# Splitting half of each plain weight quad by ScalarE and accumulating transfers in the last halves of an MLP, and an eighth mixed pair

## The chip, the cores and the metric

The kernel runs on one core of a Trainium2 chip. The metric is device time in microseconds (us) of one execution. Before the change three runs took 1934.14, 1934.61 and 1934.19 us, median 1934.19 us.

## The reference

A trunk of two layers on 256 tokens of width 2048, all in float32. Layer 0 mixes tokens by a convolution module, layer 1 by latent attention; behind each stands a squared-ReLU MLP, and the change lies in its second product alone:

```
def sq_relu_mlp(h, w1, w2):
    return jnp.square(jax.nn.relu(h @ w1)) @ w2      # 256x2048 @ 2048x8192, then @ 8192x2048
...
    h = rms_norm(x, norm_mlp_g[layer])
    x = x + sq_relu_mlp(h, mlp_w1[layer], mlp_w2[layer])
return rms_norm(x, final_norm_g)
```

## The kernel before, in words

**Split operands.** TensorE multiplies float32r operands, so each float32 value is held as a rounded upper part and a lower part. ScalarE writes the upper part of a weight tile (`hi`), VectorE subtracts it from the loaded weights (`raw`) and writes the lower part (`lo`). `mm3` (L203 to L205) makes one product of three matmuls: upper by upper, lower input by upper weight, upper input by lower weight, in this order.

**The MLP** (`mlp`, L609) runs in two halves of the 8192 hidden columns. A half has an up product (L655, L656: eight groups g of four hidden chunks of 128) and then a down product. The turned, normalised input of the up product stands in the tiles `xt`; in the last half nobody reads it after the up product. Between the two, each finished group is squared and split (L673 to L687).

**The down product of a half** has 32 chunks of 128 rows of w2, taken in pairs: 16 pairs. The output has four column blocks of 512, and two of them are made together by one `Sums` (n = 0, then n = 2). One pair by two column blocks is a *quad*: one load of 1 MB on SP's queue into one of three `raw` buffers. A quad is either

- *plain* (`Sums.plain`, L559): 8 products of `mm3`, so 24 matmuls, with two tiles of 128x1024 split by L170 (ScalarE) and L174 (VectorE); or
- *mixed* (`Sums.mixed`): 7 products, so 21 matmuls, by sums of weight blocks and of input blocks that make a 2x2 block product out of seven. Its weight blocks are prepared by `mixed_weights` (L490): four splits (L497 ScalarE, L498 VectorE) and three differences made in `raw` by VectorE (L505, L506, L507).

`MIXED` lists which pairs are mixed: eight of 16 in three of the four halves, and seven (0, 1, 4, 5, 8, 9, 12) in the last half of layer 1. `HEAD` and `TAIL` keep plain quads at both ends of a `Sums`; in n = 0 the order is two plain, two mixed, plain, two mixed, plain and so on. I call the quads of one `Sums` p0, p1, ... (plain) and m0, m1, ... (mixed).

In the last half of layer 1 the second `Sums` (n = 2) is made by `product_A` (L417), which takes plain chunks in units of four rows by one column block, so that columns 2 and 3 end one after the other; `between` puts the mixed quads among the units of column block 2. Behind it come the residual adds and the final norm.

**What sets the order.** The tile framework gives each engine its own order of instructions; an engine takes them in that order and waits by semaphores. The buffers set how far VectorE and ScalarE run ahead of TensorE: six `hi` and six `lo` tiles (`WB`), three `raw` buffers (`load`, L153). SP issues a load when the last reader of the buffer's earlier content is done. Transfers that add into what stands in SBUF are issued by GpSimd (POOL); before the change it issues them only in `Sums.put` (L578), for sums of 128x512.

Of the kernel before, what the change touches and what calls it, by code (L numbers as in the profile page):

```python
# [10 lines left out]
F32 = mybir.dt.float32  # L11
# [27 lines left out]
PAD_RIGHT = 48  # L39
PAD_KV = 8  # L40
PAD_O = 56
WB = 6
# [37 lines left out]
def trunk_kernel(  # L80
# [335 lines left out]

    def product_A(  # L417
        w, k_lo, nk, hi, lo, add, prepare, blocks=range(NNB), due=(), finish=None, before=None,
        units=None, banks=None, begun=None, beside=None, room=None,
    ):  # L420

        due = list(due)
        units = [list(range(4 * u, 4 * u + 4)) for u in range(nk // 4)] if units is None else units
        begun = set() if begun is None else begun
        nu = len(units)

        def first(ps):
            fresh = id(ps) not in begun
            begun.add(id(ps))
            return fresh  # L430

        for n in blocks:
# [12 lines left out]
            for u, ks in enumerate(units):  # L445
                if u == 0 and beside is not None:
                    beside(n, -1, due)
                wjs.append(load_split([rows(w, k_lo + ks[0], len(ks), n * NB, NB)], len(ks)))
                if u < nu - n_end:
                    for j, k in enumerate(ks):  # L450
                        for t in range(T):
                            mm3(ps[t], hi(k, t), lo(k, t), *wjs[u](j), first(ps[t]), u == nu - 1 and k == ks[-1])
                if banks is None:
                    while due:
                        prepare(due.pop(0))
                    step(-(-20 * 4 // nk) + 1 if nk > 4 * NNB else 6)
                elif n == blocks[-1]:
                    for _ in range(len(due) if n_end else min(1, len(due))):
                        prepare(due.pop(0), out=room)
                if beside is not None:  # L460
                    beside(n, u, due)
            if n_end:
                before()
                for t in range(T):


                    halves = t == T - 1
                    for u in range(nu - n_end, nu - halves):
                        products(u, t, not halves)
                    add(n, ps, t)  # L470
                    if not halves:
                        prepare(n, t)
                    else:
                        h = NB // 2
                        for c in range(2):
                            o = acc_tile()[:, :h]
                            for j, k in enumerate(units[-1]):
                                wh, wl = (w[:, c * h : (c + 1) * h] for w in wjs[-1](j))
                                mm3(o, hi(k, t), lo(k, t), wh, wl, j == 0, k == units[-1][-1])
                            add(n, {t: o}, t, c)  # L480
                            prepare(n, t, c)
                    finish(t)
            else:
                for t in range(T):
                    add(n, ps, t)
                due.append(n)
        while due:
            prepare(due.pop(0))
# [23 lines left out]
    def mixed_inputs(v, fh, fl):  # L512
# [15 lines left out]
        nc.vector.tensor_tensor(a12, a12, a11, op=ALU.subtract)  # L528
        halves(a, 3, 4)

    class Sums:


# [25 lines left out]
        def plain(self, w, k, hi, lo, k0, end, middle=None):  # L559

            at_j = split(load([rows(w, k, 2, self.n * NB, 2 * NB)], 2), nc.vector)
            order = [(j, c, t) for j in range(2) for c in range(2) for t in range(T)]
            if end:
                order.sort(key=lambda r: r[1:])
            for i, (j, c, t) in enumerate(order):
                if middle is not None and 2 * i == len(order):
                    middle()
                wh, wl = (a[:, c * NB : (c + 1) * NB] for a in at_j(j))
                ps = self.e[t][c]
                mm3(ps, hi(k0 + j, t), lo(k0 + j, t), wh, wl, self.first(ps), end and j == 1)  # L570
# [34 lines left out]
                        self.put(t, c, o)  # L605

    put_off = []

    def mlp(layer, ssq, next_gain, finish=None, before=None, beside=None, after_up=None):  # L609

        with ExitStack() as cx:
# [22 lines left out]
            for hf in range(HALVES):  # L634
# [72 lines left out]
                split_end = last and finish is not None  # L707
                for n in range(0, NNB - 2 * split_end, 2):
                    sums = Sums(n, not last or split_end)
                    ks = [2 * p for p in ps]  # L710
                    at, head = 0, HEAD[n // 2]
                    for i, k in enumerate(ks):
                        upto = (len(ms) * (i - head + 1) + (head > 1) * (len(ks) - head - TAIL)) // (len(ks) - head - TAIL + 1)
                        while at < min(upto, len(ms)):
                            mixed_quad(sums, at)
                            at += 1
                        if i == len(ks) - TAIL + 1:
                            sums.join(room)
                        at_end = i == len(ks) - 1
                        sums.plain(  # L720
                            w, k_lo + k, hi, lo, k, at_end,
                            (lambda: [prepare(due.pop(0), out=room, rest=rest) for _ in range(len(due))]) if at_end else None,
                        )
                    sums.close(room)
                    while rest:
                        rest.pop(0)()
                    if last:
                        due += [n, n + 1]
                if last and not split_end:
                    put_off.extend(lambda n=n: prepare(n) for n in due)  # L730
                if split_end:
                    sums = Sums(NNB - 2, False)
                    n2 = NNB - 2
                    units = [list(range(4 * g, 4 * g + 4)) for g in plain]
                    units[1:1] = [[2 * p, 2 * p + 1] for p in ps if p // 2 in mixed]
                    nu, at_ = len(units), [0]

                    def between(n, u, due):
                        if n == n2 and u < nu - 1:
                            while at_[0] < min(len(ms), -(-len(ms) * sum(map(len, units[: u + 1])) // sum(map(len, units[:-1])))):  # L740
                                mixed_quad(sums, at_[0])
                                at_[0] += 1
                        if n == n2 and u == nu - 1:
                            sums.join(room)

                    if after_up is not None:
                        after_up()
                    product_A(
                        w, k_lo, nkh, hi, lo, add, prepare, range(n2, NNB), due,
                        finish=(lambda t: finish(nssq, t)) if finish is not None else None,  # L750
                        before=lambda: before(nssq),
                        units=units, banks={n2 + c: [sums.e[t][c] for t in range(T)] for c in range(2)},
                        begun=sums.begun, beside=between, room=room,
                    )
            return nssq

# [1099 lines left out]
    with ExitStack():  # L1856
        gfs = []

        def load_gf():
            gfs.append(right_pool("gf", 1).tile([P, D], F32, name="gf"))  # L1860
# [83 lines left out]
```

## Time and profile before

| | |
|---|---|
| runs, median | 1934.19 us |
| the profiled execution, from its first to its last instruction | 1932.5 us |
| TensorE (PE) busy | 1921.0 us |
| VectorE (DVE), ScalarE (ACT), GpSimd (POOL) busy | 1592.2, 1095.6, 249.0 us |
| read from HBM | 363.68 MB |
| last half of layer 0: up product, down product | 641.3 to 818.8 us, 818.8 to about 980 us |
| last half of layer 1: up product, down product and end | 1582.3 to 1759.8 us, 1759.8 to 1932.5 us |

The profile has one row for an engine, a group of equal instructions or a stretch of time. A row of the timeline gives start, duration, engine, line, operation, out<-in, and in brackets the engine's idle time before it with what ended it. Times count from the start of the span. Matmuls overlap: a row of 0.39 us starts some 0.23 us after the one before it.

### The profile page before, as it was taken

What the parts mean: (1) busy time and instruction counts of PE and PEld (TensorE: products, weight loads), DVE (VectorE), ACT (ScalarE), POOL (GpSimd) and SP (SyncE); (2) the same over time, 40 slices, a digit from 0 to 9 for tenths busy, and PEclk for the clock granted to TensorE, in tenths of its full rate; (3) what the DMA queues carried; (4) which work ended last, traced back from release to release, by engine and by line L of the source; (5) the groups of instructions that cost most, each with busy time, mean ns of one, the idle gap of its engine ahead of it and who ended that gap; (6) DMA issues with size and microseconds to landing.
All of it is one profiled execution on the core that took longest, in us unless ns stands there. A gap on an engine that the chain in (4) does not pass through costs nothing.

```text
span 1932.5 us, 28477 instructions
## 1 busy us (share of the span) xinstructions
PE 1921.0 (99%) x10725; PEld 1681.5 (87%) x10725; DVE 1592.2 (82%) x2457; ACT 1095.6 (57%) x1636; POOL 249.0 (13%) x208
## 2 busy tenths in 40 slices
PE   9999999999999999999999999999999999999998
PEld 8999888888888888888898998888888888888887
DVE  7999988877999776799976766877789987678998
ACT  5667755554555545555576655555555554455554
POOL 6999200000010100000001420000000010000000
PEclk9999999999999999999999999999999999999999
DMA  7766456665585866655656545465646776665774
GB/s 230 214 183 189 153 189 206 193 194 177 175 251 194 263 195 187 194 174 196 217 176 175 142 134 192 155 216 186 188 162 225 222 248 212 191 196 175 231 219 150
DMA packets 230427, 375.50 MB, mean 194 GB/s; under 512 B 16392, under 2 KB 107792, under 8 KB 230032
## 3 DMA queue, kind: packets, MB, share of 16 engines
q1 hardware_dynamic: 224640, 363.28, 58.7%
q0 software_dynamic: 4320, 7.87, 2.2%
q10 hardware_dynamic: 1328, 2.52, 0.4%
q8 instruction: 84, 1.38, 0.3%
q14 instruction: 55, 0.45, 0.1%
HBM read 363.68 MB, written 2.10 MB: 189 GB/s over the span
## 4 chain that ended last, share of the span: by engine, by line
PE 97%; DVE 2%; DMA 0%; ACT 0%; issue 0%; ACTq 0%; DVEq 0%
PE acc L655 24%; PE acc L205 15%; PE acc L203 15%; PE acc L204 15%; PE acc L656 13%; PE acc L823 8%; PE acc L1287 2%; DVE sum L910 1%; DMA xs<-in_x 0%; PE acc L1535 0%; PE acc L1566 0%; PE acc L1565 0%; PE acc L1536 0%; PE acc L1564 0%; PE acc L1537 0%; PE tr L267 0%
## 5 line engine op out<-in xcount | busy, mean ns | idle before, releaser
L174 DVE TENSOR_TENSOR lo<-raw,hi 128x1024 fp32r<-128x1024 f32 (+2 forms) x509 | 602.2, 1197 | 232.3 <-ACT hi L170 226.6
L170 ACT ACTIVATE hi<-raw 128x1024 fp32r<-128x1024 f32 (+2 forms) x574 | 583.9, 1036 | 361.1 <-PE acc L655 203.7
L655 PE MATMUL acc<-xt,hi 128*128 128x512 f32 x2048 | 710.6, 390 | 0.0
L656 PE MATMUL acc<-xt,lo 128*128 128x256 f32 x2048 | 577.5, 282 | 0.0
L655 PEld LDWEIGHTS acc<-xt,hi 128*128 128x128 f32 x2048 | 384.3, 188 | 80.7
L656 PEld LDWEIGHTS acc<-xt,lo 128*128 128x128 f32 x2048 | 387.1, 189 | 0.2
L497 ACT ACTIVATE hi<-raw 128x1024 fp32r<-128x1024 f32 x248 | 228.7, 948 | 228.3 <-DVE raw L505 134.0
L498 DVE TENSOR_TENSOR lo<-raw,hi 128x1024 fp32r<-128x1024 f32 x248 | 263.9, 1087 | 27.6 <-ACT hi L497 22.5
L203 PE MATMUL acc<-hi,sh 128*128 128x512 f32 x514 | 200.1, 389 | 0.0
L205 PE MATMUL acc<-lo,sh 128*128 128x512 f32 x514 | 200.1, 389 | 0.0
L203 PE MATMUL acc<-hi,gh 128*128 128x512 f32 (+1 forms) x516 | 200.0, 388 | 0.0
L205 PE MATMUL acc<-lo,gh 128*128 128x512 f32 (+1 forms) x516 | 199.9, 387 | 0.0
L204 PE MATMUL acc<-hi,gl 128*128 128x512 f32 (+1 forms) x516 | 199.9, 387 | 0.0
L823 PE MATMUL acc<-xt,hi 128*128 128x256 f32 x1024 | 180.2, 281 | 0.3 <-ACT b L1106 0.2
L204 PE MATMUL acc<-hi,sl 128*128 128x512 f32 x450 | 175.1, 389 | 0.0
L578 POOL DMA_DIRECT2D xs<-v x30 | 26.5, 994 | 1136.4 <-DVE lo L174 703.2
L910 DVE SCALAR_TENSOR_TENSOR sum<-ub,w_dw,sum 128x256 f32<-128x256 f32 x409 | 164.3, 481 | 3.6 <-ACT sum L880 3.0
L174 POOL TENSOR_TENSOR lo<-raw,hi 128x1024 fp32r<-128x1024 f32 x65 | 155.0, 2410 | 17.3 <-ACT hi L170 17.3
L823 PEld LDWEIGHTS acc<-xt,hi 128*128 128x128 f32 x1024 | 154.8, 188 | 1.1 <-ACT xt L1090 0.6
L823 PE MATMUL acc<-xt,lo 128*128 128x256 f32 x512 | 139.2, 279 | 0.0
L205 PEld LDWEIGHTS acc<-lo,sh 128*128 128x128 f32 x514 | 96.5, 188 | 20.4 <-DVE lo L498 0.3
L204 PEld LDWEIGHTS acc<-hi,gl 128*128 128x128 f32 x516 | 96.9, 188 | 19.9
(314 smaller groups left out, 2531.3 us busy)
## 6 DMA issues: line engine op xcount, KB each, us to landing
raw<-in_mlp_w SPq DMA_DIRECT2D x255, 1024.0 KB, 5.5
raw<-in_conv_w_pw SPq DMA_DIRECT2D x62, 512.0 KB, 5.1
raw<-in_conv_w_pw SPq DMA_DIRECT2D x16, 1024.0 KB, 5.1
raw<-in_mla_w_o SPq DMA_DIRECT2D x16, 1024.0 KB, 5.7
raw<-in_mla_w_kv_up SPq DMA_DIRECT2D x32, 256.0 KB, 3.9
xs<-v POOLq DMA_DIRECT2D x30, 256.0 KB, 7.8
raw<-in_mla_w_in SPq DMA_DIRECT2D x8, 576.0 KB, 3.8
raw<-in_mla_w_in SPq DMA_DIRECT2D x4, 1024.0 KB
```

Source lines behind the costliest of these rows:

```text
L170: nc.scalar.activation(hi, raw[:, js, :], AF.Copy)
L174: eng.tensor_tensor(lo, raw, hi.bitcast(F32), op=ALU.subtract)
L203: nc.tensor.matmul(ps, sh, mh, start=start, stop=False)
L204: nc.tensor.matmul(ps, sl, mh, start=False, stop=False)
L205: nc.tensor.matmul(ps, sh, ml, start=False, stop=stop)
L497: nc.scalar.activation(hi, src, AF.Copy)
L498: nc.vector.tensor_tensor(lo, src, hi.bitcast(F32), op=ALU.subtract)
L655: nc.tensor.matmul(ps[b], wh[:, bs], xhl(k), start=k == 0, stop=False)
L656: nc.tensor.matmul(ps[b][:, :S], wl[:, bs], xh(k), start=False, stop=k == KC - 1)
L823: nc.tensor.matmul(pss[c][b][:, :S], w[i][:, bs], (xh, xl)[j](k), start=k == i + j == 0, stop=end and k == k0 + nk - 1 and (i, j) == terms ...
L910: nc.vector.scalar_tensor_tensor(out=out, in0=ubs[c][:, w : w + S], scalar=tap(c, w), in1=base, op0=ALU.mult, op1=ALU.add)
L1287: nc.tensor.matmul(ps2[b][t], x_kt(k, t), w[:, bs], start=k == g == i == 0, stop=k == KC - 1 and i == len(group) - 1,)
```

## The change

Four edits, all in the last half of each layer's MLP, except the table's:

1. `MIXED`: the last half of layer 1 gets pair 13 as an eighth mixed pair.
2. `side_parts`: for a plain quad, the second of its two tiles is no longer split through `hi` and `lo`. ScalarE writes -raw, rounded, into `l`; GpSimd issues a transfer that reads the same weights from HBM again and adds them onto `l`, which leaves the lower part; ScalarE writes the upper part `h` in a second operation. The first tile is split as before.
3. This is done one quad ahead in the program: `side_parts` of a plain quad, its load too, stands before the quad that precedes it. p0 is left out, and in layer 0's n = 2 the last two. In layer 1's `product_A` the three plain units behind mixed quads of column block 2 are done so, each before the mixed quad that precedes it. These are 12 quads in layer 0 and 10 in layer 1.
4. `h` and `l` (tags sideh, sidel; three buffers each) stand where `xt` stood; `xt` is opened again for the next stage in layer 0, and the final gain `gf` moves into the same pool in layer 1.

```diff
-MIXED = {(layer, half): (0, 1, 4, 5, 8, 9, 12) + (13,) * (layer + half < 2) for layer in range(2) for half in range(2)}
+MIXED = {(layer, half): (0, 1, 4, 5, 8, 9, 12, 13) for layer in range(2) for half in range(2)}
+SIDE_BUFS, SIDE_LEAD = 3, 1
...
+    def side_parts(src, pool):
+
+        _, nj, cols = src.shape
+        half = nj // 2
+        raw = load([src], nj)
+        h, l = (pool.tile([P, half, cols], F32R, tag=f"side{c}", name=nm(f"side{c}")) for c in "hl")
+        nc.scalar.activation(l, raw[:, half:, :], AF.Copy, scale=-1.0)
+        nc.gpsimd.dma_start(l, src[:, half:, :], accum_op=ALU.add)
+        nc.scalar.activation(h, raw[:, half:, :], AF.Copy)
+        both = [split_half(raw, 0, nc.vector), (h, l)]
+        return lambda j: tuple(a[:, j % half, :] for a in both[j // half])
...
-            at_j = split(load([rows(w, k, 2, self.n * NB, 2 * NB)], 2), nc.vector)
+            at_j = split(load([rows(w, k, 2, self.n * NB, 2 * NB)], 2), nc.vector) if second is None else second
...
+                    for j in range(SIDE_LEAD):
+                        look(j)
+                    for j, (kind, i) in enumerate(work):
+                        look(j + SIDE_LEAD)
...
+                            upto = min(len(ms), -(-len(ms) * sum(map(len, units[: u + 1])) // sum(map(len, units[:-1]))))
+                            while at_[0] < upto:
+                                if at_[0] == upto - 1 and len(units[u + 1]) == 4:
+                                    ks = units[u + 1]
+                                    seconds[n, u + 1] = side_parts(rows(w, k_lo + ks[0], 4, n * NB, NB), side)
```

ScalarE's order at the end of layer 0's last up product. `v<-acc` are the last reads of the up product, `hi<-raw` of L497 belong to mixed quad m0 (raw_8422) and m1 (raw_8464). Before:

```order
L673 ACTIVATE v_8327<-acc_8153 128x256
L673 ACTIVATE v_8327<-acc_8154 128x256
L673 ACTIVATE v_8336<-acc_8155 128x256
L497 ACTIVATE hi_8428<-raw_8422 128x512
L673 ACTIVATE v_8336<-acc_8156 128x256
L686 ACTIVATE gh_8325<-v_8327 128x512
L686 ACTIVATE gh_8325<-v_8336 128x512
L497 ACTIVATE hi_8435<-raw_8422 128x1024
```

The same place now; raw_8358 is p1, raw_8429 is m0, raw_8471 is p2:

```order
L698 ACTIVATE v_8327<-acc_8153 128x256
L698 ACTIVATE v_8327<-acc_8154 128x256
L698 ACTIVATE v_8336<-acc_8155 128x256
L502 ACTIVATE hi_8442<-raw_8429 128x1024
L698 ACTIVATE v_8336<-acc_8156 128x256
L542 ACTIVATE sidel_8361<-raw_8358 128x1024
L544 ACTIVATE sideh_8360<-raw_8358 128x1024
L711 ACTIVATE gh_8325<-v_8327 128x512
L502 ACTIVATE hi_8446<-raw_8429 128x1024
L542 ACTIVATE sidel_8474<-raw_8471 128x1024
```

The two side operations of p1 now stand right behind the last read of the up product, because they write where `xt` stood.

TensorE's order in p1, the second quad of the same down product, now. hi_8365 and lo_8366 are its first tile, sideh_8360 and sidel_8361 its second:

```order
L205 MATMUL acc_8353<-hi_8365,gh_7125 128x512
L206 MATMUL acc_8353<-hi_8365,gl_7126 128x512
L207 MATMUL acc_8353<-lo_8366,gh_7125 128x512
L205 MATMUL acc_8350<-sideh_8360,gh_7125 128x512
L206 MATMUL acc_8350<-sideh_8360,gl_7126 128x512
L207 MATMUL acc_8350<-sidel_8361,gh_7125 128x512
L205 MATMUL acc_8352<-sideh_8360,gh_7125 128x512
```

Nothing has moved here: the lower part of the second tile is read by the third matmul behind the quad's middle, where lo_8395 was read before.

ScalarE's order at mixed quad m1 (raw_17260) of layer 1's last half, now; raw_17368 is p3 and raw_17326 is m2:

```order
L502 ACTIVATE hi_17262<-raw_17260 128x1024
L502 ACTIVATE hi_17266<-raw_17260 128x512
L542 ACTIVATE sidel_17371<-raw_17368 128x1024
L502 ACTIVATE hi_17273<-raw_17260 128x1024
L502 ACTIVATE hi_17277<-raw_17260 128x1024
L502 ACTIVATE hi_17328<-raw_17326 128x1024
```

The side operation of p3 has come between the second and the third split of m1; p3's load goes into the buffer that p2 leaves.

More of the change, by code (lines that the diff above doesn't have):

```diff
@@ L447, in product_A @@
                     beside(n, -1, due)
-                wjs.append(load_split([rows(w, k_lo + ks[0], len(ks), n * NB, NB)], len(ks)))
+                if seconds is not None and (n, u) in seconds:
+                    wjs.append(seconds[n, u])
+                else:
+                    wjs.append(load_split([rows(w, k_lo + ks[0], len(ks), n * NB, NB)], len(ks)))
                 if u < nu - n_end:
@@ L557, in mixed, with ahead, plain @@
                 mm3(ps, fh[:, i, :], fl[:, i, :], wh, wl, self.first(ps), end and any(ps is u for u in self.u))
-        def plain(self, w, k, hi, lo, k0, end, middle=None):
-            at_j = split(load([rows(w, k, 2, self.n * NB, 2 * NB)], 2), nc.vector)
+        def ahead(self, w, k, pool):
+            return side_parts(rows(w, k, 2, self.n * NB, 2 * NB), pool)
+        def plain(self, w, k, hi, lo, k0, end, middle=None, second=None):
+            at_j = split(load([rows(w, k, 2, self.n * NB, 2 * NB)], 2), nc.vector) if second is None else second
             order = [(j, c, t) for j in range(2) for c in range(2) for t in range(T)]
@@ L707, in mlp @@
                 split_end = last and finish is not None
+                side = side_pool(f"side{layer}") if last else None
                 for n in range(0, NNB - 2 * split_end, 2):
@@ L711, in mlp @@
                     at, head = 0, HEAD[n // 2]
+                    work = []
                     for i, k in enumerate(ks):
@@ L714, in mlp, with look @@
                         while at < min(upto, len(ms)):
-                            mixed_quad(sums, at)
+                            work.append(("mixed", at))
                             at += 1
+                        work.append(("plain", i))
+                    seconds = {}
+                    def look(j):
+                        if side is None or j >= len(work) or work[j][0] == "mixed":
+                            return
+                        i = work[j][1]
+                        if i > 0 and (n == 0 or i < len(ks) - TAIL):
+                            seconds[i] = sums.ahead(w, k_lo + ks[i], side)
+                    for j in range(SIDE_LEAD):
+                        look(j)
+                    for j, (kind, i) in enumerate(work):
+                        look(j + SIDE_LEAD)
+                        if side is not None and n == j == 0:
+                            nc.gpsimd.memset(side.tile([P, PAD_SIDE], F32, name=nm("pad_side"), bufs=1), 0.0)
+                        if kind == "mixed":
+                            mixed_quad(sums, i)
+                            continue
                         if i == len(ks) - TAIL + 1:
@@ L719, in mlp @@
                         at_end = i == len(ks) - 1
+                        if at_end and side is not None and due:
+                            open_xt(f"xt{layer}b")
                         sums.plain(
-                            w, k_lo + k, hi, lo, k, at_end,
+                            w, k_lo + ks[i], hi, lo, ks[i], at_end,
                             (lambda: [prepare(due.pop(0), out=room, rest=rest) for _ in range(len(due))]) if at_end else None,
+                            seconds.get(i),
                         )
```

15 lines of the change are left out of this document (9 added, 6 removed).

## The prediction, made before the changed kernel ran

> **What bounds the kernel now.** First the page: the span, the busy shares, and the chain of work that ended last.
>
> ```profile
> span 1932.5 us, 28477 instructions
> ...
> PE 1921.0 (99%) x10725; PEld 1681.5 (87%) x10725; DVE 1592.2 (82%) x2457; ACT 1095.6 (57%) x1636; POOL 249.0 (13%) x208
> ...
> PE 97%; DVE 2%; DMA 0%; ACT 0%; issue 0%; ACTq 0%; DVEq 0%
> ```
>
> TensorE is busy 99% of the span. A busy matmul need not run at its pace, so next the stretches of the two last down products, for the number of matmuls.
>
> ```profile
> 840.00:860.00 20.00, 20.00 (x90) 16.57 (x89) 19.60 (x22) 10.85 (x12) 0.00 (x0) 1.00 0.66 232
> 860.00:880.00 20.00, 20.00 (x90) 16.53 (x90) 19.71 (x21) 12.80 (x15) 0.00 (x0) 1.00 0.55 177
> ...
> 1780.00:1800.00 20.00, 20.00 (x90) 16.53 (x89) 19.51 (x21) 11.21 (x12) 0.00 (x0) 1.00 0.72 242
> 1880.00:1900.00 20.00, 20.00 (x90) 16.57 (x89) 19.71 (x22) 12.48 (x17) 0.00 (x0) 1.00 0.65 215
> ```
>
> The columns are PE, PEld, DVE, ACT, POOL, granted clock, DMA share and GB/s. Ninety matmuls begin in every 20 us, at full clock: there is no gap to win. VectorE stands at 19.5 to 19.7 of 20 and just keeps up, so relieving it gains nothing by itself; only fewer matmuls do.
>
> **The eighth pair.** It turns 24 matmuls into 21 in both `Sums` of layer 1's last half, so six go. Their pace is read at the start of layer 0's last down product:
>
> ```profile
> 818.66 0.28 PE L656 MATMUL acc<-xt,lo 128*128 128x256 f32 x1
> 818.78 0.39 PE L203 MATMUL acc<-hi,gh 128*128 128x512 f32 x1
> ...
> 824.23 0.39 PE L203 MATMUL acc<-hi,gh 128*128 128x512 f32 x1
> ...
> 827.40 0.39 PE L205 MATMUL acc<-lo,gh 128*128 128x512 f32 x1
> ```
>
> From 818.78 to 824.23 lie the 24 matmuls of p0: 0.227 us each. Six are **-1.4 us**. The extra inputs of pair 13 are made during the up product, where VectorE idles over a quarter of the time (13.94 of 20 us from 1740 to 1760); I cost them at nothing.
>
> ```profile
> 1740.00:1760.00 20.00, 20.00 (x117) 17.76 (x116) 13.94 (x22) 10.06 (x15) 0.00 (x0) 1.00 0.59 187
> ```
>
> **The split, away from the ends.** Per quad, by these groups (mean ns behind the comma):
>
> ```profile
> L498 DVE TENSOR_TENSOR lo<-raw,hi 128x1024 fp32r<-128x1024 f32 x35 | 42.4, 1222 | 4.3 <-ACT hi L497 3.6
> L497 ACT ACTIVATE hi<-raw 128x1024 fp32r<-128x1024 f32 x35 | 36.6, 1057 | 47.2 <-DVE raw L505 33.5 <-DVE raw L507 6.7 <-PE acc L204 3.1
> L174 DVE TENSOR_TENSOR lo<-raw,hi 128x1024 fp32r<-128x1024 f32 x19 | 22.5, 1219 | 0.5 <-ACT hi L170 0.5
> L170 ACT ACTIVATE hi<-raw 128x1024 fp32r<-128x1024 f32 x20 | 19.9, 1045 | 2.8 <-DMA raw<-in_mlp_w 2.8
> ```
>
> A plain quad loses one subtraction of VectorE (1.22 us) and gains one ScalarE operation (some 1.05 us), one transfer of 0.5 MB and one issue on POOL's queue. ScalarE idles 7 of 20 us or more in the stretches above and POOL has nothing else there, so 22 such quads cost nothing on the path once the work runs ahead. What is late next would be the transfer; in the alternating part it has the preceding mixed quad, 21 x 0.227 = 4.8 us, and half its own, besides the lead with which ScalarE works; I take that as cover. DMA load rises by half a load for a plain quad, from shares of 0.55 to 0.72, so the engines stay short of full.
>
> **The first side quad, in both layers.** Here the cover is missing. `l` lies where `xt` was, so ScalarE may write it only after the last matmul of the up product. Before, p1 was split long ahead: now it is made after the up product and is due at its old place, 827.40 in the rows above, 8.6 us after 818.78. ScalarE's side of it:
>
> ```profile
> 817.94 1.08 ACT L673 ACTIVATE v<-acc 128x256 f32<-128x256 f32 x3 [0.74 <-PE acc L656]
> 818.92 0.63 ACT L497 ACTIVATE hi<-raw 128x512 fp32r<-128x512 f32 x1
> 819.45 0.37 ACT L673 ACTIVATE v<-acc 128x256 f32<-128x256 f32 x1
> ```
>
> In the new order a split of 1024 columns stands between the reads: 818.92 + 1.0, the last read 0.4, the side operation 1.05: done at 821.3, POOL issues at about 821.4. The transfer then has **6.0 us**. No transfer of this kind is in the trace; the nearest are POOL's accumulating ones of half the size, out of SBUF:
>
> ```profile
> L578 POOL DMA_DIRECT2D xs<-v x30: 852/883/1342, 547.1 to 1845.4; - x30
> ...
> DMA to landing us min/median/max: 3.5/7.8/10.8
> ```
>
> The price per byte is in the queues' rows, with the share of 16 engines' time:
>
> ```profile
> q1 hardware_dynamic: 224640, 363.28, 58.7%
> q0 software_dynamic: 4320, 7.87, 2.2%
> ```
>
> q0: 0.022 x 1932.5 / 7.87 = 5.4 us per MB on all 16 engines, so the second 0.26 MB adds 1.4 us: at least 3.5 + 1.4 = 4.9, at most 10.8 + 1.4 = 12.2 us. The engines are empty at this place:
>
> ```profile
> 822.00:826.00 4.00, 4.00 (x19) 3.34 (x18) 3.99 (x7) 1.70 (x2) 0.10 (x1) 1.00 0.00 0
> 826.00:830.00 4.00, 4.00 (x19) 3.30 (x19) 2.79 (x4) 2.30 (x3) 0.00 (x0) 1.00 0.00 0
> ```
>
> Only m1's load joins, as it waits for p1's buffer, that is for sideh, at about 822.4. I take the median, 7.8 us, the quiet set against the double size: late by 1.8 us, bounds 0 and 6.2. TensorE has nothing else in its order, and so much is lost, in layer 1 as well: **+3.6 us**.
>
> The Trainium skill speaks against this wait: "DMA: Bandwidth & Descriptors", section "Anatomy of one DMA — SWDGE (gpsimd) path", gives a transfer issued by GpSimd 2.0 us and its bytes at 436 GB/s, an estimate of 3.2 us here, and then the sum is without the 3.6 us. For half the size it gives 2.6 us where the trace has 3.5 at least and 7.8 as the median, so I keep to the trace.
>
> **Behind it**, ScalarE's order puts p3's side operation ahead of m1's last splits, in layer 1 ahead of its third. p3's load waits for p2's buffer, which VectorE leaves some 10 us after the up product's end, and takes 5.5 us:
>
> ```profile
> raw<-in_mlp_w SPq DMA_DIRECT2D x255, 1024.0 KB, 5.5
> ```
>
> So that split comes at about 16 + 1 + 1 us, its subtraction at 19.4, and TensorE wants it at 10.9 + 4.8 + 10 x 0.227 = 18.0 us, plus what p1 was late. A late p1 covers it; with a punctual one it costs some 1.4 us in layer 1, about 0.9 in layer 0. It isn't added.
>
> **The end of layer 1, n = 2.** Now three mixed quads follow each other, where two did:
>
> ```profile
> 1881.38 1.22 DVE L505 TENSOR_TENSOR raw<-raw 128x1024 f32<-128x1024 f32 x1
> ...
> 1888.14 1.22 DVE L505 TENSOR_TENSOR raw<-raw 128x1024 f32<-128x1024 f32 x1
> ...
> 1890.73 2.52 DVE L498 TENSOR_TENSOR lo<-raw,hi 128x1024 fp32r<-128x1024 f32 x2
> ```
> ```profile
> 1893.60 0.39 PE L205 MATMUL acc<-lo,sh 128*128 128x512 f32 x1
> ```
>
> One mixed quad takes VectorE 6.76 us (1881.38 to 1888.14) and TensorE 4.8, so each costs 2.0 us of lead; a plain unit gives back 5.45 - 2.3 = 3.2 us as it was and 4.3 us with half its split gone, the unit of two rows that goes away gave 1.4. The last subtraction ends at 1893.25 and is used at 1893.60: 0.35 us are left before, at the point where the lead is lowest. Counted from the first run on, that point lies at -7 x 2.0 + 1.4 + 2 x 3.2 = -6.2 us. Now the lowest point is the sixth mixed quad, the end of the second run of three: -6 x 2.0 + 4.3 = -7.7 us, 1.5 deeper, so 1.1 us late on the same start. Against that, `hi` and `lo` hold one tile less of each plain quad, about 1.1 us of VectorE's work further ahead, where buffers and not VectorE set the start. Bounds 0 and 1.5; I take **+0.5 us**, near the middle.
>
> **Sum:** -1.4 + 3.6 + 0.5 = +2.7 us on the span of 1932.5, so 1935.2; the runs' median lies 1.7 above the span, and I assume that it does so again: **1936.9 us**.
>
> **Rivals.** *Late transfers (slower).* If the first transfer of a layer lands over 8.4 us after its issue, each costs over 2.4 us, and with -1.4 + 0.5 the sum passes 3.9 us, 0.2% (about what a measurement can tell from no change). For it: 7.8 us is for half the size, and 12.2 is in reach; against it, the empty engines. At 11.0 us: 2 x 5.0 - 0.9 = +9.1, 1943.3 us. *The transfer is hidden.* Landing within 6.0 us, as the fastest rows and the skill's rule have it, leaves -1.4, up to 2.3 at m1 and 0.5: 1932.8 to 1935.6, say 1934.5 us. *The side path is late all along.* Raw buffers held one quad longer and 0.5 MB more per plain quad would make each of 22 side quads wait; at 0.5 us each +11, 1946 us. Against it: cover of 4.8 us and more. *VectorE's relief pays.* That needs gaps on TensorE that the profile doesn't show; -3.9 us would be needed.
>
> **How the numbers follow.** Forecast 0.46, late transfers 0.35, hidden 0.14, late all along 0.03, relief 0.02. Faster 0.02; the same, forecast and hidden, 0.60; slower 0.38. Range: below 1933.2 lies the part of "hidden" without any wait and the relief, 0.07; above 1943.5 lie transfers at over 11 us and the late side path, 0.10.
>
> **What would show it.** In the changed profile: a gap on TensorE in p1 of both layers, ended by a DMA onto sidel, of some 1.8 us, with POOL's issue 2.6 us after the up product's end; none later in n = 0; 90 matmuls per 20 us elsewhere; VectorE below 19 of 20 in these stretches; six matmuls fewer. It is wrong if sidel lands within 6 us, if the gaps stand in later quads, or if m1's splits rather than the transfer end TensorE's wait.

## The result, and the profile after

Four runs of the changed kernel gave 1966.61 to 1970.62 us, median 1969.71, beside a median of 1934.28 for the kernel before: +35.4 us, ratio 1.0180 (95% interval 1.0166 to 1.0194). The forecast was 1936.9 us, at most 1943.5. The page of the profiled execution (1970.62 us):

```profile
span 1968.9 us, 28505 instructions
...
PE 1934.6 (98%) x10719; PEld 1684.6 (86%) x10719; DVE 1577.9 (80%) x2449; ACT 1118.6 (57%) x1662; POOL 269.0 (14%) x232
...
PE 87%; DMA 5%; DVE 3%; ACT 3%; issue 1%; ACTq 0%; SPq 0%; DVEq 0%
...
L503 DVE TENSOR_TENSOR lo<-raw,hi 128x1024 fp32r<-128x1024 f32 (+1 forms) x256 | 273.0, 1088 | 77.2 <-ACT hi L502 74.2
...
L205 PE MATMUL acc<-hi,sh 128*128 128x512 f32 x512 | 203.1, 397 | 14.1 <-ACT hi L502 14.1
```

Six matmuls fewer and less VectorE time, as meant; yet PE's part of the last chain fell from 97% to 87%. L502 and L503 are the splits of the mixed quads (L497, L498 before), and L205 is the first matmul of `mm3` (L203 before). The same two groups read before:

```profile
L498 DVE TENSOR_TENSOR lo<-raw,hi 128x1024 fp32r<-128x1024 f32 x248 | 263.9, 1087 | 27.6 <-ACT hi L497 22.5
...
L203 PE MATMUL acc<-hi,sh 128*128 128x512 f32 x514 | 200.1, 389 | 0.0
```

The engines that ran ahead now wait: VectorE for ScalarE (74.2 us for 22.5), TensorE for both. The stretches 840 to 880, 1780 to 1800 and 1880 to 1900, shown of before, read now, with the one from 880 to 900 beside them:

```profile
840.00:860.00 20.00, 16.65 (x59) 13.17 (x60) 14.47 (x15) 11.57 (x13) 1.01 (x2) 0.83 0.62 184
860.00:880.00 20.00, 20.00 (x90) 16.56 (x89) 16.53 (x17) 13.27 (x16) 1.57 (x2) 1.00 0.76 211
880.00:900.00 20.00, 17.87 (x78) 14.06 (x76) 14.86 (x16) 11.38 (x13) 1.74 (x2) 1.00 0.80 239
1780.00:1800.00 20.00, 14.62 (x62) 11.10 (x60) 9.25 (x11) 7.00 (x10) 0.89 (x1) 0.98 0.84 263
1880.00:1900.00 20.00, 16.64 (x55) 11.87 (x54) 19.42 (x21) 10.67 (x13) 0.86 (x1) 0.83 0.86 255
```

Instead of 90 matmuls, 55 to 78 begin in a bad stretch, and in two of them the granted clock is 0.83. All of the loss lies in the two last down products. From the first matmul of the down product to the first of the next stage layer 0 took 160.7 us before and 176.8 after; to the program's last matmul layer 1 took 164.6 and 184.4. What lies between the two was 780.3 and 780.5 us. I call these two lengths **L0** and **L1**.

**The forecast wait is there.** TensorE's timeline at p1 of layer 0:

```profile
827.07 0.39 PE L205 MATMUL acc<-sideh,gh 128*128 128x512 f32 x1
827.30 0.39 PE L206 MATMUL acc<-sideh,gl 128*128 128x512 f32 x1
828.92 0.50 PE L207 MATMUL acc<-sidel,gh 128*128 128x512 f32 x1 [1.24 <-DMA sidel<-in_mlp_w]
```

1.62 us from start to start instead of 0.23: 1.4 us lost, the same at 1784.56 in layer 1. GpSimd issued at 821.72, and the transfer landed 7.16 us later.

**The next one is not.** TensorE again, 12 us on, at mixed quad m1:

```profile
839.26 0.39 PE L207 MATMUL acc<-lo,sh 128*128 128x512 f32 x1
842.83 0.50 PE L205 MATMUL acc<-hi,sh 128*128 128x512 f32 x1 [3.19 <-ACT hi L502]
843.16 0.41 PE L206 MATMUL acc<-hi,sl 128*128 128x512 f32 x1
844.09 0.80 PE L207 MATMUL acc<-lo,sh 128*128 128x512 f32 x1 [0.52 <-DVE lo L503]
844.68 0.63 PE L205 MATMUL acc<-hi,sh 128*128 128x512 f32 x1
845.11 0.63 PE L206 MATMUL acc<-hi,sl 128*128 128x512 f32 x1
```

and ScalarE at the same time:

```profile
835.28 1.06 ACT L502 ACTIVATE hi<-raw 128x1024 fp32r<-128x1024 f32 x1 [1.93 <-DVE raw L510]
839.83 1.06 ACT L542 ACTIVATE sidel<-raw 128x1024 fp32r<-128x1024 f32 x1 [3.49 <-DMA raw<-in_mlp_w]
840.79 1.04 ACT L544 ACTIVATE sideh<-raw 128x1024 fp32r<-128x1024 f32 x1
841.74 2.51 ACT L502 ACTIVATE hi<-raw 128x1024 fp32r<-128x1024 f32 x3
```

m1's last split is the first of the three at 841.74. It stands behind the side operation of p3, which waits for p3's load. That load was issued at 828.38 and took 11.4 us; 4 MB of loads and transfers were asked for between 821.7 and 828.4.

**It goes on like this.** The chain of waits from 879 to 901, in order of time:

```profile
879.38 6.05 DMA raw<-in_mlp_w
...
885.51 0.51 ACT sidel L542
...
886.48 1.04 ACT sideh L544
887.52 0.95 ACT hi L502
...
888.50 1.23 DVE lo L503
...
889.75 6.90 DMA raw<-in_mlp_w
...
896.73 0.06 ACT sidel L542
...
897.70 1.05 ACT hi L502
...
898.77 1.24 DVE lo L503
...
900.02 9.30 DMA raw<-in_mlp_w
```

This is a loop: the load of a side quad; ScalarE's side operations, which waited for it; the mixed quad's last split behind them; VectorE's subtraction, which frees the mixed quad's raw buffer; the next side quad's load, which waited for that buffer. The two turns shown are a load plus 4.3 and 3.4 us, 10.4 and 10.3 us in all, where a plain and a mixed quad take TensorE 45 x 0.227 = 10.2. The next two stretches from load to load, 13.6 and 11.3 us, are no turns of this loop: there it is the plain quad's own split by VectorE (L176) that frees the buffer. In these 45.5 us TensorE lost 4.6. No sidel was waited for there: apart from the p1s, the transfers landed 3.7 to 19 us ahead of their use, 5.8 us after their issue in the median.

### The profile page after: what moved, and what is told of

Its sections match the earlier page's. It is cut to its first block, busy times and chain, and to the rows that moved or that the text cites. A ratio compares the mean times of both kernels' runs of the same rounds, so it can differ in the third digit from the quotient of the medians.

```text
span 1968.9 us, 28505 instructions
## 1 busy us (share of the span) xinstructions
PE 1934.6 (98%) x10719; PEld 1684.6 (86%) x10719; DVE 1577.9 (80%) x2449; ACT 1118.6 (57%) x1662; POOL 269.0 (14%) x232
## 4 chain that ended last, share of the span: by engine, by line
PE 87%; DMA 5%; DVE 3%; ACT 3%; issue 1%; ACTq 0%; SPq 0%; DVEq 0%
PE acc L680 23%; PE acc L681 12%; PE acc L207 12%; PE acc L205 12%; PE acc L206 12%; PE acc L877 8%; DMA raw<-in_mlp_w 5%; PE acc L1341 2%; DVE sum L964 1%; ACT hi L502 1%; DVE lo L503 1%; ACT sideh L544 1%; DVE lo L176 0%; DMA xs<-in_x 0%; PE acc L1589 0%
## 5 line engine op out<-in xcount | busy, mean ns | idle before, releaser
L176 DVE TENSOR_TENSOR lo<-raw,hi 128x1024 fp32r<-128x1024 f32 (+2 forms) x481 | 571.6, 1200 | 231.0 <-ACT hi L172 227.1
L172 ACT ACTIVATE hi<-raw 128x1024 fp32r<-128x1024 f32 (+2 forms) x546 | 557.8, 1038 | 344.0 <-PE acc L680 195.3
L502 ACT ACTIVATE hi<-raw 128x1024 fp32r<-128x1024 f32 (+1 forms) x256 | 236.2, 947 | 225.5 <-DVE raw L510 120.9
L503 DVE TENSOR_TENSOR lo<-raw,hi 128x1024 fp32r<-128x1024 f32 (+1 forms) x256 | 273.0, 1088 | 77.2 <-ACT hi L502 74.2
L205 PE MATMUL acc<-hi,sh 128*128 128x512 f32 x512 | 203.1, 397 | 14.1 <-ACT hi L502 14.1
L205 PE MATMUL acc<-hi,gh 128*128 128x512 f32 (+1 forms) x428 | 166.7, 389 | 0.0
L206 PE MATMUL acc<-hi,gl 128*128 128x512 f32 (+1 forms) x428 | 166.4, 389 | 0.0
L207 PE MATMUL acc<-lo,gh 128*128 128x512 f32 (+1 forms) x428 | 166.4, 389 | 0.0
L176 POOL TENSOR_TENSOR lo<-raw,hi 128x1024 fp32r<-128x1024 f32 x65 | 154.9, 2406 | 17.5 <-ACT hi L172 17.5
L205 PEld LDWEIGHTS acc<-hi,sh 128*128 128x128 f32 x512 | 97.5, 190 | 37.2 <-ACT hi L502 17.8
```

The lines of the kernel that those rows point to most:

```text
L172: nc.scalar.activation(hi, raw[:, js, :], AF.Copy)
L176: eng.tensor_tensor(lo, raw, hi.bitcast(F32), op=ALU.subtract)
L205: nc.tensor.matmul(ps, sh, mh, start=start, stop=False)
L206: nc.tensor.matmul(ps, sl, mh, start=False, stop=False)
L207: nc.tensor.matmul(ps, sh, ml, start=False, stop=stop)
L502: nc.scalar.activation(hi, src, AF.Copy)
```

## The experiments

Theories. **Order**: in ScalarE's queue the side operation stands ahead of the preceding mixed quad's last splits and waits for its load. **Early load**: the side quad's load takes one of three raw buffers a quad too soon. **Traffic**: the transfers slow the loads. **Late transfer**: TensorE waits for sidel itself. All lengths in us; the time is a median where there were several runs, and L0 and L1 come from one profile each. How far they scatter can be seen in layer 0, where e_side is the same kernel as the changed one: 175.2 and 176.8. A difference of some 2 us between two kernels with side quads is therefore no evidence by itself.

| kernel | L0 | L1 | time |
|---|---|---|---|
| before | 160.7 | 164.6 | 1934.2 |
| changed | 176.8 | 184.4 | 1969.7 |
| e_pair: eighth pair alone | 160.5 | 167.8 | 1937.95 (11 runs) |
| e_side: side path alone | 175.2 | 188.0 | 1972.6 (4 runs) |
| e_traffic: old splits, unread transfers | 161.3 | 174.6 | 1945.6 |
| e_copy: the same, plain copies | 160.5 | 170.8 | 1940.1 |
| e_late: loads in old order | 172.6 | 178.8 | 1961.4 |
| e_mend: side operations behind the splits | 204.9 (+15.2, see below) | 220.6 | 2049.9 |
| e_nat: both | 201.5 | 209.8 | 2020.5 |
| e_vec: side quads without transfers | 165.6 | 175.3 | 1950.3 |
| e_own: one raw buffer of their own, layer 0 | 174.8 | 184.2 | 1968.5 |
| e_from3: side quads from the fourth on | 167.3 | 177.4 | 1954.1 |
| e_own2: that, two own buffers, layer 0 | 164.6 | 177.9 | 1951.6 |
| e_own2v: that, without transfers | 162.8 | 175.6 | 1947.4 |
| e_p1: p1 the only side quad | 162.2 | 174.2 | 1945.4 |
| e_gps: pair, GpSimd subtracts nine halves | 160.5 | 174.0 | 1943.8 (5 runs) |

**The pair alone (e_pair)**: before, with the new `MIXED`.

> The kernel before with the eighth pair alone, no side quads. All theories on the side path agree that its loss of some 36 us needs the side path: 1932.9 us if the pair costs nothing (six matmuls x 0.227 = -1.4), up to 1934.0 if the second run of three mixed quads in n = 2 makes TensorE wait 0.5 to 1.1 us. A rival that blames the pair for layer 1's larger loss (19.8 us against 16.0 in layer 0) gives 1936 us or more.

1937.95 us, ratio 1.0018 (1.0009 to 1.0027). The theories had expected 1934.0 us at most and the rival that blames the pair 1936 or more, so the pair does cost something by itself. Without any side path TensorE waits for splits in n = 2, from 1859.03 to 1898.04 (3.6 us in six gaps of 0.4 to 0.8). The pair adds 14 instructions and 8.1 us to VectorE (1600.3 for 1592.2 us), which had nothing to spare there. It is no gain.

**The transfers alone (e_traffic)**

```diff
-            at_j = split(load([rows(w, k, 2, self.n * NB, 2 * NB)], 2), nc.vector) if second is None else second
+            src = rows(w, k, 2, self.n * NB, 2 * NB)
+            at_j = split(load([src], 2), nc.vector)
+            if second is not None:
+                extra(at_j.second, src, second)
```

`extra` writes -hi into `l` by ScalarE and issues the accumulating transfer onto it. The same is done in `product_A`.

> The changed kernel with the plain quads split by VectorE as before, at their old place, and beside that ScalarE's extra operation (a negated copy, made from the split's own hi, so that it cannot stand ahead of it) and the accumulating transfer of 0.5 MB, into tiles that nobody reads. Theory traffic (the accumulating transfers slow the weight loads) expects most of the loss: 1955 to 1970 us. Theory order (ScalarE's side operation stands ahead of the mixed quad's last splits and waits there for its own load) and theory early load (the plain quad's load takes one of three raw buffers a quad too soon) expect 1933 to 1938 us.

The time, 1945.6 us, lies between the two forecasts. L0 is 161.3: in layer 0 the traffic alone costs 0.6 us, though the loads take 7.0 us in the median (5.8 before, 6.6 in the changed kernel). The crowd at the start is not in this run: p2's transfer is issued at 840.08, not at 825.08 as in the changed kernel. In layer 1 it costs 6.7 on top of the pair's 3.2, which no theory expected; the largest gap there, 3.4 us at 1850.54, ends with a subtraction some 8 us into n = 2. Its cause is open. The trace also shows what the transfers would have done had anyone waited: issued where ScalarE comes to them in the old order, all but each layer's first landed 6 to 10 us after TensorE had used that half.

**Side operations behind the splits, loads early (e_mend) or in old order (e_nat)**

```diff
-        nc.scalar.activation(l, raw[:, half:, :], AF.Copy, scale=-1.0)
+        if col is not None:
+            nc.scalar.activation(col, last_hi[0], AF.Copy, scale=0.0, bias=1.0)
+        nc.scalar.activation(h, raw[:, half:, :], AF.Copy, scale=1.0 if col is None else col)
+        nc.scalar.activation(l, h.bitcast(F32), AF.Copy, scale=-1.0)
         nc.gpsimd.dma_start(l, src[:, half:, :], accum_op=ALU.add)
-        nc.scalar.activation(h, raw[:, half:, :], AF.Copy)
...
```

The rest of the edit moves the calls. `h` is now made first and `l` from it, so the transfer also starts one ScalarE operation later.

> The changed kernel, with the loads one quad ahead as there, but ScalarE's two side operations and the half that VectorE splits stand behind the last split of the mixed quad (the side operation takes its scale of 1.0 from a column that is written from that split). Theory order expects the gaps in the later quads to go and only the first side quads' waits to stay (1.4 us each and what follows there): 1936 to 1945 us. Theory early load expects 1955 us or more, since the raw buffers are taken as in the changed kernel; theory traffic expects the same, 1960 to 1970 us. Theory late transfer expects new gaps ended by sidel, since the transfers start later.

> The side path with the loads in their old order and with ScalarE's two side operations held behind the mixed quad's last split. If the 2049.9 us of the kernel with early loads came from the transfers (issued some 1 to 2 us ahead of their use and landing after 9 to 10 us), this one is slow as well, 1990 to 2050 us, with TensorE waiting for sidel in most side quads. If it came from the early loads in three raw buffers, this one gives 1940 to 1965 us.

No theory had so long a time for e_mend, by 80 us and more; the gaps ended by sidel, 68.5 us in 17 side quads, are those that theory late transfer expected. (The next stage's first matmul comes in the midst of e_mend's down product, so 15.2 us of its loss lie behind L0.) e_nat, within the first range given for it, shows the same without the early loads. Who waited for the transfer in e_nat:

```profile
L556 POOL DMA_DIRECT2D sidel<-in_mlp_w x22: 859/869/1228, 822.9 to 1977.0; - x22
...
PE acc L207: 58.0, 16
...
DMA to landing us min/median/max: 5.5/8.5/13.0
```

TensorE stood 58 us, in 16 side quads, for transfers issued 1.8 to 7.4 us, mostly 4 to 5, before it was ready for them. So the overtaking in the changed kernel gives the transfer the start that it needs, and then ScalarE waits for the load. With three raw buffers, either the transfer was late or the splits were. In e_mend ScalarE waits for loads as well:

```profile
ACT hi L502 <- DMA raw<-in_mlp_w: 38.3, 9, 9.4
```

**Loads in old order (e_late)**: `SIDE_LEAD = 0`. The three side quads of `product_A` keep their early loads.

> The changed kernel with SIDE_LEAD = 0: the side quad's load and split are asked for at the quad's own place, so loads and raw buffers go round in their old order, but ScalarE's side operations still stand ahead of the mixed quad's last one to three splits, as in the changed kernel. Theory early load expects most of the loss to go: 1934 to 1942 us. Theory order alone (the side operation's wait for its load is what counts, whichever way the loads go round) expects 1950 to 1970 us. Theory traffic expects 1960 to 1970 us, theory late transfer more than the changed kernel's 1969.7.

1961.4 us, within the ranges of order alone and of traffic: L0 and L1 lose 4.2 and 5.6 us less. The early loads are a smaller part; ScalarE still waited 17.7 us for side loads in layer 0's stage (19.3 in the changed kernel).

**No transfers (e_vec)**

```diff
-        nc.scalar.activation(l, raw[:, half:, :], AF.Copy, scale=-1.0)
-        nc.gpsimd.dma_start(l, src[:, half:, :], accum_op=ALU.add)
         nc.scalar.activation(h, raw[:, half:, :], AF.Copy)
+        nc.vector.tensor_tensor(l, raw[:, half:, :], h.bitcast(F32), op=ALU.subtract)
```

> The changed kernel with early loads and the side tiles in their place and order, but the subtraction on VectorE; no accumulating transfer and one ScalarE operation less. If the loads' order and ScalarE's waiting for them are enough by themselves, both last halves stay long (172 us or more and 180 us or more; 1960 us or more). If it needs the transfers' traffic, which lengthens the loads (median 6.6 us against 5.8), they fall to 162 to 168 us and 168 to 175 us: 1937 to 1950 us.

The time and L1 (175.3) lie just above the second forecast's ranges, L0 inside. With order and buffers as in the changed kernel but without transfers, L0 is 165.6: of 16.0 us lost 4.9 stay. Beside e_traffic's 0.6 neither part explains the loss alone: most of it needs both. How they act together is argued and not shown apart: the transfers lengthen the load (median in layer 0's stage 6.6 us in the changed kernel, 6.1 here, 5.8 before) and add a ScalarE operation, and where the load lies in the loop that counts; p1's wait for its transfer goes as well.

**Own raw buffers (e_own, e_own2), the start (e_from3)**

```diff
+            raw = pool.tile([P, nj, cols], F32, tag="sraw", name=nm("sraw"), bufs=1)
...
-                        if i > 0 and (n == 0 or i < len(ks) - TAIL):
+                        if i > 2 - n and (n == 0 or i < len(ks) - TAIL):
```

The first line is e_own's (in e_own2 with `bufs=2`), the second pair e_from3's and e_own2's.

> The changed kernel, but in layer 0 the load of a side quad (from the third on) goes into a raw buffer of its own where xt was; layer 1 is untouched. If the loss comes from side loads that stand in the ring of three raw buffers and from ScalarE waiting there for them, layer 0's last half (160.7 us before, 176.8 us changed) falls to 162 to 168 us and the time to 1955 to 1961 us, with layer 1's last half still at 184 us. If it comes from transfer traffic or from the transfers' own time, layer 0 stays at 174 us or more, and the time at 1967 us or more.

> The changed kernel with side quads only from the fourth plain quad of n = 0 on (four side quads fewer). If the start, where raw buffers wait for the up product's end, is a loss of its own, the waits at p1 (1.4 us a layer) and the cluster of gaps and slow matmuls behind it (7 us in layer 0, 8 us in layer 1) go: about 1952 to 1956 us. If each run of side quads makes its own loss wherever it begins, the cluster moves to the fourth plain quad: 1960 to 1968 us.

> Side quads from the fourth plain quad on, as in the run that gave 167.3 us for layer 0's last half, and there the side quads' loads go into two raw buffers of their own (side tiles two deep instead of three). With one own buffer the loop was a load of 7 to 8.4 us and some 4 us of splits, 11 to 13 us a side quad where TensorE needs 10.3; with two it is halved. If a loop of load and splits through the raw buffers sets the pace, layer 0's last half falls to 160.5 to 163 us, with layer 1 as it was (177 us), and the time to about 1949 us. If the traffic or the transfers' time is the limit, layer 0 stays at 166 us or more.

e_own missed: 174.8, the figure that its rival, traffic or transfer time, had given; by itself it does not speak for the loop. The rows give another reading: one buffer makes a loop of its own, since the next load waits until VectorE has left the last one; its side loads were issued at 875.87, 888.63 and 899.97, 11 to 13 us apart, as long as the turn that it replaced. e_from3 came out as the first theory had it (1954.1 us): two side quads fewer at each layer's start take 9.4 and 6.9 us off, 59% of layer 0's loss. There the raw buffers stand full until the up product ends, and then 4 MB are asked for at once. Of the 6.6 us left in L0, e_own2 takes 2.8, between its two forecasts, and ScalarE's wait for the load is gone. From e_from3's waits (stretch 840 to 987):

```profile
ACT sidel L542 <- DMA raw<-in_mlp_w: 17.6, 9, 5.5
```

From e_own2's groups (stretch 820 to 985):

```profile
L546 ACT ACTIVATE sidel<-sraw 128x1024 fp32r<-128x1024 f32 x10 | 10.4, 1045 | 0.6 <-DMA sraw<-in_mlp_w 0.6
```

**e_own2 without transfers (e_own2v)**: e_vec's edit on top.

> Two own raw buffers in layer 0 and side quads from the fourth on, but with the subtraction on VectorE and without transfers. If what was left in layer 0 with two own buffers (164.6 us against 160.7 before) comes from the accumulating transfers, layer 0 goes to 160.5 to 162 us. If it comes from side tiles only two deep or from the changed order of the splits, it stays at 163.5 us or more.

162.8, between the two: 1.7 of the 3.8 us left go with the transfers, 2.1 stay. What the 2.1 are is open; the side tiles are only two deep there. Taken apart in this order, layer 0's 16.0 us are 9.4 for the first two side quads, 2.8 for the shared raw buffers, 1.7 for the transfers and 2.1 open; the last three are hardly above the scatter. Of layer 1's loss these runs take only the start apart.

**p1 alone (e_p1)**: `if i == 1 and n == 0`, none in `product_A`.

> The changed kernel with p1 of n = 0 as its only side quad in each layer, and the eighth pair. The prediction's own terms for p1 give 1.4 us in layer 0 (162 us for the last half) and 1.4 on top of the pair's in layer 1 (169 us): 1940 to 1941 us. If the start's cluster of gaps needs only p1, layer 0 has 166 us or more; if it needs the second side quad behind it, p2, it has 163 us or less.

L0 162.2, as the prediction's own term had it: the cluster needs the second side quad. In layer 1 p1 alone cost more, so that L1 is 174.2 and the time 1945.4 us, above the forecast:

```profile
1769.64 0.39 PE L206 MATMUL acc<-sideh,gl 128*128 128x512 f32 x1
1773.64 0.80 PE L207 MATMUL acc<-sidel,gh 128*128 128x512 f32 x1 [3.61 <-DMA sidel<-in_mlp_w]
1774.24 0.63 PE L205 MATMUL acc<-sideh,gh 128*128 128x512 f32 x1
```

GpSimd issued at 1764.06 and ScalarE issued `gf`'s 1 MB at 1764.10; sidel landed 9.5 us later instead of 7.2. In the changed kernel `gf` comes 3 us behind. The prediction had not counted `gf`; that it is what lengthened the transfer is likely, and no run without it shows it.

**Plain copies (e_copy)**: e_traffic without `accum_op`.

> The kernel with old splits and the unread transfers (1945.6 us), the transfers now a plain copy of the same 0.5 MB. If accumulating is what makes them long (5.5 us alone, 9.7 us in the median beside loads), they land in 3 to 6 us now; if it is the loads beside them, they stay at 8 us or more.

Both halves of the guess were partly right: the median falls from 9.6 to 7.7 us, the shortest from 5.5 to 3.9. So both the loads beside them and the adding make them long. The share of 16 engines' time between 820 and 985 shows what the adding does for the same bytes. e_traffic:

```profile
q0 software_dynamic: 1728, 6.29, 19.7%
```

e_copy:

```profile
q0 software_dynamic: 1728, 6.29, 9.8%
```

**The pair with relief from GpSimd (e_gps)**: `nc.gpsimd` in place of `nc.vector` for the second half of nine plain quads in layer 1.

> No side path; the eighth pair, and in layer 1's last half the subtraction of the second half of the alternating plain quads (nine of them) on GpSimd, which took 2.41 us for one of this size elsewhere in the kernel. If the pair alone came out slower (1937.95 us) because VectorE ran out of time, this relief brings the six matmuls' 1.4 us to light: 1932.5 to 1933.5 us. If GpSimd's result comes late or VectorE's operations become longer beside it, 1935 to 1942 us.

1943.77 us, ratio 1.0047 (1.0033 to 1.0061): worse than the pair alone, and above both forecasts. VectorE's groups between 1765 and 1925 in e_pair:

```profile
L498 DVE TENSOR_TENSOR lo<-raw,hi 128x1024 fp32r<-128x1024 f32 x47 | 56.7, 1220 | 4.0 <-ACT hi L497 3.0
```

in e_gps:

```profile
L498 DVE TENSOR_TENSOR lo<-raw,hi 128x1024 fp32r<-128x1024 f32 x47 | 64.9, 1395 | 6.8 <-ACT hi L497 4.8 <-PE acc L204 1.0
```

**The side path alone (e_side)**: the changed kernel with the old `MIXED`.

> The side path alone, with the seven mixed pairs that layer 1's last half had before. If the two parts of the change add up (side path 16.0 us in layer 0, where the pairs are the same before and after, and 16.5 us in layer 1, the changed kernel's excess over the pair alone), 1965 to 1968 us. If the third mixed quad in a row is what lets the side path fail in layer 1, layer 1's last half falls below 175 us: 1960 us or less.

1972.59 us, ratio 1.0198 (1.0181 to 1.0215), above my range. The parts don't add up: with side quads the pair takes 3.6 us off L1, without them it adds 3.2. With the old `MIXED` layer 1 has 11 side quads and not 10, one of them in the pair's place; whether that is the reason is open. It is settled that the loss is the side path's. No version beat the kernel before.

## Why the prediction was wrong

- **What bounds the kernel**: right as a reading of before, and right that relieving VectorE gains nothing by itself. That TensorE has no gaps, however, says nothing about how near the other engines are to making some.
- **The split, away from the ends, at nothing**: this is the step that failed, here and in "Behind it". "What is late next would be the transfer; in the alternating part it has the preceding mixed quad, 21 x 0.227 = 4.8 us, and half its own, besides the lead with which ScalarE works; I take that as cover." For the transfer the cover held: in the changed kernel only the two p1s waited for theirs. Away from m1 no term stood for what lies behind the side operations on ScalarE: they wait for their quad's load, and the mixed quad's last split, its subtraction and, by the freed buffer, the next load wait with them (the loop above). Away from the start layer 0 lost 6.6 us (e_from3), of which own buffers take back 2.8. Nor could the side operations have stood behind the splits, with three raw buffers: there the lead was 0.2 to 3.5 us (from GpSimd's issue to TensorE's use in e_traffic, p1s aside), and a transfer beside loads took 9.6 us in the median, 13.2 at most, so that TensorE waits for it (e_nat, 16 times). I looked only for what the side quad itself waits for.
- **DMA load "short of full"**: the average was. Between 820 and 985 the queues' shares went from 55.5% for the loads alone to 50.8 + 22.7 = 73.5% with 6.29 MB of transfers; in four of the five stretches above it is 0.76 to 0.86, and a load took up to 11.9 us (the one issued at 1858.98). I priced this at nothing, though the load sits in the loop.
- **The first side quad**: right in mechanism and size, 1.4 us each for 1.8, the issue 2.8 us after the up product for 2.6, the transfer 7.2 us for 7.8. e_p1 shows it by itself: L0 +1.5. The size is partly luck: with next to nothing beside it such a transfer took 5.5 us (e_traffic), which would just have been in time. The prediction counted one load beside it; in the changed kernel p2's transfer and another load had joined by 825.74.
- **"Behind it"**: the right mechanism, the very one that spoils the rest, named for m1 alone and priced in layer 0 with a load of 5.5 us: 0.9 us, covered by a late p1. The load took 11.4, and the place cost 3.3 + 0.7 us of waits and some 3 us of slow matmuls; with p1's own 1.4 that is most of the 9.4 us that e_from3 takes off, so this term is the largest in layer 0. That gaps stand in later quads was one of the prediction's own signs of being wrong. I should have asked whether the same order returns at every side quad; the order of the changed kernel says that it does.
- **The pair**: six matmuls went, but the waits in n = 2 were mis-sized: +0.5 against 4.6 us by itself (3.2 + 1.4).
- **The rival "late all along"** was the nearest, with a chance of 0.03 and 0.5 us a quad (its +11 us make 1945.2, not 1946). The chance rested on the same cover. The side path's loss over the pair alone is 16.3 + 16.5 us, 1.5 for each of 22 quads, though much of it is at the start.
- **The Trainium skill's rule** ("DMA: Bandwidth & Descriptors", section "Anatomy of one DMA — SWDGE (gpsimd) path"), 3.2 us for the transfer: no run agrees. A plain copy with next to nothing beside it took 3.9 us, an accumulating one 5.5, beside loads 7.7 and 9.6 in the median. Keeping to the trace was right.

## What to carry to other kernels

Before an operation that waits for a transfer is sent ahead on an in-order engine, list what stands behind it there, and follow the buffers round: where its load waits for what it blocks, a loop arises whose turn must be shorter than the bound engine's period. Price a transfer by its landing beside the traffic that will be there, and compare that with the lead of the engine that starts it, not with the time between two uses. An engine that is busy 98% of a stretch, as VectorE was here, has no room for a trade that adds only little to it.

## What the runs showed of the hardware

**A wait can cost twice.** TensorE in three stretches of the changed kernel (the column behind POOL is the granted clock):

```profile
838.00:844.00 6.00, 2.39 (x10) 1.32 (x8) 1.42 (x3) 4.17 (x5) 0.86 (x1) 0.95 0.21 25
844.00:850.00 6.00, 5.91 (x14) 4.65 (x15) 5.86 (x8) 2.82 (x4) 0.00 (x0) 0.50 0.81 244
850.00:856.00 6.00, 6.00 (x28) 4.92 (x27) 3.58 (x4) 2.18 (x3) 0.00 (x0) 0.98 0.67 208
```

After the waits of 3.2 and 0.5 us the clock is half until about 850: 13 matmuls at 0.43 us, 2.6 us lost on top. In the two last down products some 39 matmuls ran so, about 7.8 us of the 36. The Trainium skill, "TensorE: Matmul & The Clock Gate", section "Part 1: The HAM clock gate", has the array's clock halve after an idle window of about 3.4 us and come back after a busy one; the halving and 0.43 us agree. That the array must stand idle for so long is not borne out: in the changed kernel waits of 1.0 and 0.7 us (ended at 1893.21 and 1894.63) were followed by seven matmuls at 0.43 us, with this clock:

```profile
1894.80:1898.10 3.30, 3.30 (x8) 2.59 (x9) 3.30 (x4) 1.28 (x2) 0.00 (x0) 0.50 0.50 157
```

Waits of 1.6 and 0.5 us (ended at 888.52 and 889.77) were followed by none. In e_late a wait of 1.9 us (ended at 901.43) was followed by nine slow matmuls and one of 2.0 us (at 1858.07) by none. So between 1 and 2 us the length of a wait did not decide it; waits of 3 us and more, at 842.83 and 1800.99, were both followed by the half clock.

**Adding onto SBUF doubled a transfer's engine time here**: 19.7% against 9.8% of 16 engines for the same 6.29 MB (e_traffic, e_copy).

**GpSimd beside VectorE**: a subtraction of 128x1024 on VectorE takes 1.22 us, but 2.87 us (at 1867.79 in e_gps) while GpSimd subtracts. The Trainium skill, "SBUF — State Buffer", section "Who interferes with whom", says that a VectorE instruction with two SBUF inputs contends with a GpSimd instruction that reads SBUF; the trace agrees.
